# Sums of the down weights begin two pairs later in each up-projection

## The chip, the cores and the metric

The kernel runs on one core of one Trainium2 chip. The metric is device time in microseconds, from start to end of one execution. Five engines work side by side, each strictly in the order of its own instruction queue: PE (TensorE, matrix products; its weight loads are shown apart as PEld), DVE (VectorE), ACT (ScalarE), POOL (GpSimd) and SP (SyncE, which here issues the DMA transfers). An instruction whose input is not there holds up all that stands behind it on its engine.

## What is computed

The reference is one inference step of a two-layer encoder for 1024 prompt rows and 128 sample rows (1152 in all) of width 1024. Each layer is an attention block, then a channel mixer ("conv FFN"). The change lies in the channel mixer, which both layers run:

```python
def conv_ffn(h, prev, w_up, conv_w, conv_b, w_down):
    u = h @ w_up                          # 1024 -> 5632 columns
    ue = jnp.concatenate([prev, u], axis=1)
    y = conv_b
    for tap in range(CONV_W):             # 3 taps over positions
        y = y + conv_w[tap] * ue[:, tap:tap + T]
    a, g = jnp.split(y, 2, axis=-1)       # 2816 columns each
    out = (jax.nn.gelu(g) * a) @ w_down   # 2816 -> 1024
    return out, ue[:, T:]
```

## The kernel before

A float32 operand is held as a rounded part and a remainder ("hi" and "lo", made by `split`: an ACT cast at line 177, then a DVE subtraction at line 188), and each product is made of three matmuls.

**The up-projection (`ffn`, line 1213 on).** The 5632 columns are 44 blocks of 128. Block j of `a` and block j of `g` form pair j, with j from 0 to 21. Pairs 0 and 1 are `plain`: ordinary products. Pairs 2 to 21 are `spair`: each 2x2 block product is done with seven products instead of eight (`products`, line 1152), which needs sums of the two weights and sums of the input. The sums of the input are made once for each layer, by `tsums`, in the program between the plain pairs and pair 2: nine tiles go through a ring of three buffers; each is loaded (line 1131), POOL makes two subtractions (lines 1135, 1136), DVE two more (1137, 1138), ACT and DVE split the results, and only then may the buffer take the next tile. The sums of a pair's weights are four POOL operations (lines 1177 to 1180), then split for PE. PE multiplies at line 1229; the results are taken out of PSUM by ACT (1188, 1197) and DVE (1190); then come the convolution taps (`conv_row`: ACT at 1318 and 1321, DVE at 1278 and 1323, POOL at 1287), the gelu (ACT, 1330) and the gate (POOL, 1331), whose result `actD` goes to DRAM.

**Work for the down-projection inside this loop.** The down-projection (`down`) also uses seven products, so it needs sums of activations and of the down weights, both put in DRAM ahead of time. `act_sums` (POOL at 1343 to 1346, then two `actS` stores at 1348) works in place on the two gate buffers after each odd pair, and the next writer of a gate buffer (DVE, 1323) must wait for the store. `weight_sums(m)`, for m from 0 to 10, works in place in a buffer of its own, `w0`: two loads (line 1354), POOL at 1355, 1356 and 1357, and two stores to `wT` (1358, 1359). There is one such buffer, so the loads of m wait for the stores of m-1. The list `wsum` says in which pair m is called; its index in the list is m.

**Other work in the loop of layer 0.** `ada` streams modulation weights through the same load buffers as the pairs (loads at 226, PE at 234), and after pair 2 a table is unrolled to DRAM by `skew_b`, 16 DRAM-to-DRAM copies (line 1673).

**What sets the order.** The kernel is traced in program order and a scheduler then fixes one order for each engine from its own estimate of times; `issue_after` adds a constraint. So an edit moves not only its own instructions.

Of the kernel before, what the change touches and what calls it, by code (L numbers as in the profile page):

```python
# [19 lines left out]
NFF = 22  # L20
# [82 lines left out]
class Trunk:  # L103
# [1140 lines left out]
    def ffn(self, l, xsrc, xdst, affs):  # L1244
# [150 lines left out]
            gated(j, ya, y[0])  # L1395

        self.pend = []
        wsum = [2, 3] + list(range(4, NFF - 1, 2))
        for j in range(NPL):
            plain(j)  # L1400
        self.take_w0(F32)
# [534 lines left out]
```

## Time and profile before

| | us |
|---|---|
| median of 3 runs (lowest, highest) | 2820.66 (2814.4, 2827.81) |
| the profiled execution | 2813.54 |
| its span, first to last instruction | 2811.8 |
| PE busy | 2657.6 (95%) |
| DVE busy | 2031.0 (72%) |
| ACT busy | 1393.4 (50%) |
| POOL busy | 1031.4 (37%) |

Times in the trace count from the start of the span. Layer 0's up-projection runs from about 480 to 1020, layer 1's from about 2010 to 2530. A share of busy time is an average over stages; which engine waits, and for what, is read stage by stage. In a row of the timeline the columns are start, duration, engine, line, operation, output<-input, size and count, and in brackets the idle time of the engine before it and what ended it. In a row of windows they are the stretch, its length, then busy time and number of instructions of PE, PEld, DVE, ACT and POOL, the clock granted to PE (1.00 is full), the busy share of the DMA engines and GB/s.

### The profile page before, as it was taken

Reading aid. Unit: us, or ns where it says so; the run is one execution under the profiler, and the core shown is the slowest. Engines: PE = TensorE matmul, PEld = TensorE weight load, DVE = VectorE, ACT = ScalarE, POOL = GpSimd, SP = SyncE. Lnnn points to the kernel's source line nnn. Section 1 sums busy time; section 2 is a strip of 40 time slices with the busy share of each in tenths; the row PEclk is TensorE's granted clock in tenths of the full one; section 3 lists DMA queues with packets and bytes.
Section 4 is the critical chain, followed back from the end, with each engine's and each line's share of the span. In section 5 each row is a group of like instructions: output and inputs, shape, how many; then the busy total and the mean of one; then the engine's idle time right before and its main releaser. Section 6 shows DMA issues by size and latency. Waiting matters only on the chain.

```text
span 2811.8 us, 47453 instructions
## 1 busy us (share of the span) xinstructions
PE 2657.6 (95%) x17134; PEld 2341.9 (83%) x17134; DVE 2031.0 (72%) x4010; ACT 1393.4 (50%) x2912; POOL 1031.4 (37%) x808
## 2 busy tenths in 40 slices
PE   7999889989999999998899999989989999999997
PEld 5887768889999997877798888867889999997775
DVE  4376767777777785679654677767888888885668
ACT  3475724443444344455636666663444444444554
POOL 2132523456555642112420122242465656542101
PEclk9999999999999999999999999999999999999998
DMA  8756444575565557675767467764453433347664
GB/s 296 222 163 190 141 131 158 186 275 198 190 206 201 186 169 245 199 246 194 279 205 266 114 162 197 215 193 142 156 189 112 143 134 130 132 145 249 199 211 151
DMA packets 252715, 528.59 MB, mean 188 GB/s; under 512 B 40032, under 2 KB 100400, under 8 KB 252480
## 3 DMA queue, kind: packets, MB, share of 16 engines
q1 hardware_dynamic: 252480, 525.56, 56.9%
q8 instruction: 135, 2.21, 0.3%
q14 instruction: 100, 0.82, 0.1%
HBM read 391.12 MB, written 143.77 MB: 190 GB/s over the span
## 4 chain that ended last, share of the span: by engine, by line
PE 69%; DVE 11%; DMA 10%; POOL 4%; issue 3%; ACT 3%; SPq 1%; DVEq 0%; POOLq 0%; ACTq 0%
PE PS L1229 26%; PE PS L1476 15%; PE PS L319 10%; PE PS L306 7%; PE PS L602 2%; PE PS L580 2%; DVE wl L188 2%; PE PS L234 2%; PE PS L551 1%; DMA w0f<-in_wdn_dram 1%; PE PS L293 1%; DMA actS<-F 1%; DMA ws<-in_adaw_dram 1%; DVE F L518 1%; PE PS L554 1%
## 5 line engine op out<-in xcount | busy, mean ns | idle before, releaser
L1229 PE MATMUL PS<-H,wh 128*128 128x256 f32 (+1 forms) x2624 | 408.6, 298 | 0.0
L1476 PE MATMUL PS<-wh,xa 128*128 128x512 f32 x1144 | 366.5, 400 | 17.5 <-ACT wh L177 6.4
L1229 PEld LDWEIGHTS PS<-H,wh 128*128 128x128 f32 x2624 | 373.1, 192 | 0.4 <-issue 0.4
L188 DVE TENSOR_TENSOR wl<-F,wh 128x512 fp32r<-128x512 f32 (+2 forms) x278 | 274.2, 996 | 31.6 <-ACT wh L177 29.1
L1190 DVE TENSOR_TENSOR F<-PS,F 128x320 f32<-128x320 f32 (+1 forms) x446 | 196.4, 450 | 130.3 <-PE PS L1229 129.2
L1476 PEld LDWEIGHTS PS<-wh,xa 128*128 128x128 f32 x1144 | 216.9, 190 | 74.4 <-ACT wh L177 12.4
L177 ACT CAST wh<-F 128x512 fp32r<-128x512 f32 (+2 forms) x278 | 163.7, 598 | 219.4 <-PE PS L1229 132.5
L1229 PE MATMUL PS<-H,wl 128*128 128x256 f32 (+1 forms) x1312 | 234.3, 301 | 22.2 <-ACT F L1197 15.8
L1476 PE MATMUL PS<-wl,xa 128*128 128x512 f32 x572 | 228.1, 400 | 0.4 <-DVE wl L188 0.4
L1229 PEld LDWEIGHTS PS<-H,wl 128*128 128x128 f32 x1312 | 196.7, 193 | 30.8 <-ACT F L1197 16.2
L1321 ACT ACTIVATE PS<-F 128x512 f32<-128x512 f32 x160 | 124.6, 779 | 187.6 <-DVE F L1323 107.2
L188 DVE TENSOR_TENSOR xa<-xa 128x640 fp32r<-128x640 f32 (+1 forms) x154 | 128.0, 836 | 122.2 <-ACT xa L177 121.1
L1229 PE MATMUL PS<-xa,wh 128*128 128x320 f32 (+1 forms) x1328 | 203.8, 296 | 0.0
L1331 POOL TENSOR_TENSOR F<-F 128x1152 f32<-128x1152 f32 x44 | 125.6, 2855 | 188.9 <-DVE F L1323 147.7
L177 ACT CAST xa<-xa 128x640 fp32r<-128x640 f32 (+1 forms) x154 | 104.0, 682 | 178.2 <-DMA xa<-actD 118.2
L1229 PEld LDWEIGHTS PS<-xa,wh 128*128 128x128 f32 x1328 | 186.3, 189 | 0.0
L177 ACT CAST wh<-ws 128x512 fp32r<-128x512 f32 (+1 forms) x153 | 104.3, 691 | 97.8 <-PE PS L1229 30.2
L1065 POOL TENSOR_TENSOR F<-F 128x1024 f32<-128x1024 f32 x24 | 58.6, 2443 | 227.8 <-PE PS L1042 95.1
L188 DVE TENSOR_TENSOR wl<-ws,wh 128x512 fp32r<-128x512 f32 (+1 forms) x135 | 135.7, 1011 | 8.4 <-ACT wh L177 7.9
L640 POOL TENSOR_TENSOR F<-F,x2r 64x512 f32<-64x512 f32 x62 | 79.4, 1281 | 168.2 <-DVE F L616 147.2
L319 PE MATMUL PS<-xa,H 128*128 128x512 f32 x504 | 133.3, 405 | 6.2 <-ACT xa L177 3.3
L306 PE MATMUL PS<-H,w0r 128*128 128x384 f32 (+1 forms) x720 | 138.3, 342 | 0.0
(349 smaller groups left out, 6384.2 us busy)
## 6 DMA issues: line engine op xcount, KB each, us to landing
ws<-in_adaw_dram SPq DMA_DIRECT2D x64, 512.0 KB
ws<-in_wup_dram SPq DMA_DIRECT2D x49, 512.0 KB
F<-in_adaw_dram SPq DMA_DIRECT2D x48, 512.0 KB
w0f<-in_wdn_dram SPq DMA_DIRECT2D x44, 512.0 KB
actS<-F SPq DMA_DIRECT2D x44, 512.0 KB
xa<-actS SPq DMA_DIRECT2D x88, 256.0 KB
F<-in_wup_dram SPq DMA_DIRECT2D x39, 512.0 KB
xa<-actD SPq DMA_DIRECT2D x66, 256.0 KB
```

The source lines that it names most:

```text
L177: nc.scalar.copy(out, in_)
L188: self.eng(el).tensor_sub(lo, src, hi.bitcast(F32))
L234: mm = nc.tensor.matmul(ps[32 * j : 32 * j + 32, hf * 256 : hf * 256 + 256], self.cT[:, k * 32 : k * 32 + 32], w[:, j * 256 : j * 256 + 25 ...
L306: mm = self.nc.tensor.matmul(out[:, 0:n], w[a][:, k * 128 : k * 128 + 128], H[:, p, k, s0 : s0 + n], start=i == 0, stop=i == 23)
L319: self.nc.tensor.matmul(out[:, 0:n], H[:, p, j * kn + k, t0 : t0 + 128], w[a][:, k * n : k * n + n], start=i == 0, stop=i == 23,)
L640: self.eng("v" if last else "p").tensor_mul(on[r, q], on[r, q], rb[r, :])
L1065: self.eng(er[0]).tensor_mul(xr, x, self.lng)
L1190: nc.vector.tensor_add(d, v(ps), a if len(a.shape) == 3 else v(a))
L1229: self.pairmm = nc.tensor.matmul(ps[:, 0:m], w[a][:, k * 128 : k * 128 + 128], x(p, k, n), start=start and c == 0, stop=c == 11, skip_grou ...
L1321: nc.scalar.activation(ps, u[:, 2 + o : 514 + o], AF.Identity, **aff)
L1331: nc.gpsimd.tensor_mul(yg, yg, ya)
L1476: self.downmm = nc.tensor.matmul(ps, a[p][:, i * 128 : i * 128 + 128], w[q], start=first and c == 0, stop=last and c == 2, skip_group_chec ...
```

## The change

The list `wsum` is replaced; nothing else.

```diff
@@ ffn @@
         self.pend = []
-        wsum = [2, 3] + list(range(4, NFF - 1, 2))
+        wsum = list(range(4, 9)) + list(range(10, NFF - 1, 2))
         for j in range(NPL):
             plain(j)
```

With NFF = 22 the list was 2, 3, 4, 6, 8, 10, ..., 20 and is now 4, 5, 6, 7, 8, 10, ..., 20. Both have eleven entries. Sums 0, 1 and 2 move from pairs 2, 3, 4 to pairs 4, 5, 6; sum 3 moves from pair 6 to pair 7; sums 4 to 10 stay. Pairs 2 and 3 lose their sums, pairs 5 and 7 gain one. This holds in both layers. Each sum moved is four DMAs on SP's queue (two loads of 512 KB, stores of 256 and 512 KB) and three POOL operations on 128x512.

What it does to the order is seen at two places.

POOL at the start of layer 0's up-projection, from the sixth tile of `tsums` on. Before (L1135 and L1136 are the tile subtractions, w0f is the buffer of the weight sums, L1331 is the gate of pair 0):

```order
L1135 TENSOR_TENSOR F<-F 128x4x64
L1136 TENSOR_TENSOR F<-F 128x4x64
L1355 TENSOR_TENSOR w0f<-w0f 128x512
L1331 TENSOR_TENSOR F<-F 128x1152
L1356 TENSOR_TENSOR w0f<-w0f 128x512
L1135 TENSOR_TENSOR F<-F 128x4x64 x3
L1357 TENSOR_TENSOR w0f<-w0f 128x512
L1136 TENSOR_TENSOR F<-F 128x4x64 x3
```

Now:

```order
L1135 TENSOR_TENSOR F<-F 128x4x64
L1287 TENSOR_TENSOR F<-F 128x8x2
L1136 TENSOR_TENSOR F<-F 128x4x64
L1331 TENSOR_TENSOR F<-F 128x1152
L1135 TENSOR_TENSOR F<-F 128x4x64 x2
L1136 TENSOR_TENSOR F<-F 128x4x64
L1135 TENSOR_TENSOR F<-F 128x4x64
L1136 TENSOR_TENSOR F<-F 128x4x64 x2
```

The three operations of sum 0 are gone from between the tile subtractions, and the second subtraction of one tile now stands ahead of the last tile. Layer 1 has the same rows at its start.

SP's queue in layer 0 from the second weight load of pair 3 (L1376) to the first of pair 4 (L1375); skb<-eb are the copies of the table, actS the activation sums. Before:

```order
L1376 DMA ws<-in_wup_dram 128x1024
L1354 DMA w0f<-in_wdn_dram 128x1024 x2
L226 DMA F<-in_adaw_dram 128x1024
L1673 DMA skb<-eb 128x1x768 x9
L1348 DMA actS<-F 128x1024
L1673 DMA skb<-eb 128x1x768 x2
L226 DMA ws<-in_adaw_dram 128x1024
L1358 DMA wT_104<-w0f 128x512
L1673 DMA skb<-eb 128x1x768
L1348 DMA actS<-F 128x1024
```

Now:

```order
L1376 DMA ws<-in_wup_dram 128x1024
L226 DMA F<-in_adaw_dram 128x1024
L1673 DMA skb<-eb 128x1x768 x9
L1348 DMA actS<-F 128x1024
L1673 DMA skb<-eb 128x1x768 x3
L1348 DMA actS<-F 128x1024
L226 DMA ws<-in_adaw_dram 128x1024
L1673 DMA skb<-eb 128x1x768
L226 DMA F<-in_adaw_dram 128x1024
L1673 DMA skb<-eb 128x1x768 x3
L226 DMA ws<-in_adaw_dram 128x1024
L1375 DMA ws<-in_wup_dram 128x1024
```

Both loads of sum 1 and its stores are gone from this stretch, and the two activation stores stand nearer to its start.

ACT in layer 0 from the gelu (L1330) that stood ahead of the first weight casts of pair 4 (L177 CAST wh<-ws) on, before:

```order
L1318 ACTIVATE F<-F 128x128
L1291 COPY F<-F 128x18
L1321 ACTIVATE PS<-F 128x512
L1330 ACTIVATE F<-F 128x1152
L177 CAST wh<-ws 128x512 x2
L177 CAST wh<-F 128x512
```

Now:

```order
L1318 ACTIVATE F<-F 128x128
L1291 COPY F<-F 128x18
L177 CAST wh<-ws 128x512 x2
L1321 ACTIVATE PS<-F 128x512
L177 CAST wh<-F 128x512 x2
L1318 ACTIVATE F<-F 128x128
```

The casts of pair 4's weights no longer stand behind the last convolution steps of pair 3 and its gelu.

## The prediction

> **What bounds the kernel now.** I read the page first, then the windows of the two up-projections, PE's waits in the opening of each, and there the timelines of POOL, DVE, ACT and SP. In the first fence are windows:
>
> ```profile
> 607.00:1010.00 403.00, 403.00 (x3159) 373.03 (x3160) 306.31 (x475) 169.49 (x320) 240.76 (x184) 1.00 0.58 196
> 2104.00:2530.00 426.00, 419.82 (x3127) 418.03 (x3125) 370.80 (x547) 198.51 (x376) 239.64 (x183) 1.00 0.39 134
> ...
> 533.80:540.64 6.84, 0.00 (x0) 0.00 (x1) 6.41 (x14) 6.01 (x12) 0.00 (x0) 0.79 0.49 154
> 540.64:581.80 41.16, 40.73 (x308) 38.26 (x312) 26.43 (x41) 13.42 (x26) 19.48 (x17) 0.95 0.80 274
> 581.80:584.08 2.28, 0.41 (x9) 0.01 (x1) 2.06 (x4) 0.05 (x1) 0.52 (x1) 1.00 1.06 385
> 584.08:593.60 9.52, 9.50 (x64) 8.28 (x64) 5.43 (x13) 2.18 (x5) 2.36 (x2) 0.82 1.01 371
> 593.60:597.83 4.23, 0.00 (x0) 0.00 (x0) 3.99 (x7) 4.23 (x8) 3.31 (x4) 0.75 0.83 315
> 597.83:612.00 14.17, 13.12 (x82) 12.31 (x83) 12.57 (x11) 4.38 (x9) 11.32 (x7) 0.83 0.51 165
> ...
> 2063.00:2072.00 9.00, 0.08 (x2) 0.04 (x1) 8.57 (x18) 7.32 (x15) 2.77 (x5) 0.72 0.56 203
> ```
>
> From 607 on layer 0 is bound by PE alone: 403.00 busy of 403.00 us. There nothing that POOL or the DMAs gain or lose reaches the end while PE stays fed. Layer 1 loses 6.2 us of 426. What is not PE's own time lies in the openings: in layer 0 three stops, at 533.8, 581.8 and 593.6, and in layer 1 one of 8.9 us at 2063. After each stop the clock is lower for some microseconds (0.95, 0.82, 0.83), which lengthens the matmuls. PE's waits in the opening of layer 0, and then of layer 1:
>
> ```profile
> PE PS L1229 <- ACT F L1197: 6.9, 1, 6.9
> PE PS L1229 <- DVE wl L188: 5.7, 3, 4.2
> PE PS L1229 <- DVE F L1190: 1.9, 1, 1.9
> ...
> PE PS L1229 <- ACT F L1197: 8.9, 1, 8.9
> PE PS L1229 <- DVE F L1190: 4.6, 5, 2.6
> ```
>
> **Term A, the opening of both layers.** PE stands at 533.8 because ACT's copy L1197 comes only at 540.17. It queues behind the last casts of the input sums, and those hang on POOL and DVE (timelines, layer 0):
>
> ```profile
> 516.29 1.48 POOL L1355 TENSOR_TENSOR w0f<-w0f 128x512 f32<-128x512 f32 x1
> 518.74 2.68 POOL L1331 TENSOR_TENSOR F<-F 128x1152 f32<-128x1152 f32 x1 [0.97 <-ACT F L1330]
> 521.38 1.47 POOL L1356 TENSOR_TENSOR w0f<-w0f 128x512 f32<-128x512 f32 x1
> 528.29 0.74 POOL L1135 TENSOR_TENSOR F<-F 128x256 f32<-128x256 f32 x1 [3.68 <-DVE F L1278]
> 528.99 1.29 POOL L1357 TENSOR_TENSOR w0f<-w0f 128x512 f32<-128x512 f32 x1
> 530.24 2.31 POOL L1136 TENSOR_TENSOR F<-F 128x256 f32<-128x256 f32 x3
> ...
> 516.53 1.52 DVE L1137 TENSOR_TENSOR F<-F 128x256 f32<-128x256 f32 x1
> 518.08 0.42 DVE L1138 TENSOR_TENSOR F<-F 128x256 f32<-128x256 f32 x1
> 518.99 4.15 DVE L188 TENSOR_TENSOR xa<-F,xa 128x256 fp32r<-128x256 f32 x2 [0.48 <-ACT xa L177]
> 523.06 0.96 DVE L188 TENSOR_TENSOR x2r<-F,x2r 128x256 fp32r<-128x256 f32 x1
> 531.01 0.94 DVE L1137 TENSOR_TENSOR F<-F 128x256 f32<-128x256 f32 x1 [0.82 <-POOL F L1136]
> ...
> 524.05 0.32 SPq L1131 DMA_DIRECT2D F<-hD  x1
> 540.17 0.69 ACT L1197 COPY F<-PS 128x320 f32<-128x320 f32 x2
> ```
>
> Two things are seen. While POOL runs L1355, a DVE subtraction of the size that takes 0.42 takes 1.52; and two such take 4.15, to 523.1, while POOL runs L1331 and then L1356. And the last tile is loaded at 524.05, when the subtraction of 523.06 (0.96 long) has freed its buffer. Without sum 0, DVE comes free after L1331, at 521.4 instead of about 522.9: 1.4 us sooner, and so does the last load. Its first subtraction then comes at about 526.9, L1357's 1.29 us behind it are gone, and one of the three L1136 (0.77 each) stands ahead now: POOL ends 1.4 + 1.3 + 0.8 = 3.5 us sooner. DVE, which works nearly without a pause from 524 to 538, follows by less: its start is 1.4 sooner, the pause of 0.82 goes, and of the long 0.96 at 523.06 some 0.2 goes too. That is 2.4, and ACT's chain to L1197 follows DVE one for one. Bounds: 0 (DVE and ACT take no less time in another order) and 4.2, the whole of 1.48 + 1.47 + 1.29. I take 2.4, since DVE is the later of the two. Layer 1 has the same operations and the longer stop: twice 2.4 = 4.8 us. Both stops stay over 4 us, so the low clock behind them stays.
>
> The Trainium skill, page "SBUF — State Buffer", section "SBUF: two separate sides", says that DVE and GpSimd share one pair of ports, and that whichever starts first holds it for a whole instruction, the other blocking. The rows of 1.52 and 4.15 agree. By that rule alone each of the three operations would be given back whole, 4.2 us a layer, and term A would be 8.5 us; it also holds for the same operations in pairs 5 and 7.
>
> **Term B, the crowded DMA of layer 0.** From about 555 to 595 the DMA engines are full. Windows, then SP's rows, then the chain of waits, then the sizes:
>
> ```profile
> 560.00:580.00 20.00, 19.57 (x149) 18.81 (x149) 16.18 (x21) 8.32 (x17) 12.64 (x11) 1.00 1.03 361
> 554.48 0.90 SPq L1354 DMA_DIRECT2D w0f<-in_wdn_dram  x2
> 556.53 9.00 SPq L1673 DMA_DIRECT2D skb<-eb  x9
> 583.19 0.33 SPq L1375 DMA_DIRECT2D ws<-in_wup_dram  x1
> 566.23 9.25 DMA actS<-F
> 575.50 0.76 DVE F L1323
> 583.53 0.50 DVE F L1190
> w0f<-in_wdn_dram SPq DMA_DIRECT2D x44, 512.0 KB
> wT<-w0f SPq DMA_DIRECT2D x22, 512.0 KB
> wT<-w0f SPq DMA_DIRECT2D x22, 256.0 KB
> ```
>
> Sum 1 is issued into this: 1024 + 512 + 256 = 1792 KB, 1.84 MB, at 361 GB/s 5.1 us of full DMA. Its two loads (2.9 us) stand ahead of everything. The activation store needs 9.25 us to land, so DVE's L1323 (the convolution of pair 2, into the buffer just stored) starts at 575.50, and PE's next evict L1190 waits in DVE's queue until 583.53: the second stop, 2.28 - 0.41 = 1.87 us. With term A's 2.4 and the 2.9 us the store lands about 5 us sooner, while PE arrives only 2.4 sooner. The slack of 2.9 covers the 1.87: the stop goes, and the slow stretch behind it (9.52 us at 0.82: 1.7 us) with it. Together 3.6 us. Bounds: 0 and 3.6.
>
> On that slow stretch the Trainium skill, page "TensorE: Matmul & The Clock Gate", section "What's actually happening", says the clock falls after an idle window of about 3.4 us. Here 0.82 follows a stop of 1.87 us, so the row and not the page is used; by the page this term would be 1.9.
>
> **Term C, the third stop.** At 593.6 PE waits for pair 4's weights. Their cast stands behind pair 3's last convolution steps and gelu; in the new order it stands ahead of them, so it is bound by the landing of the weights. These are issued at 583.19 after 1.84 MB less and with PE 2.4 us ahead; they wait also for a buffer that PE's ada matmuls free just before 581.8, so I reckon issue at 579, landing at 584 to 585 (the crowd is through by then), cast and split by 586.5. PE would be there at 593.6 - 2.4 - 1.87 - 1.7 = 587.6. So the stop of 4.23 goes, with the slow clock behind it (14.17 us at 0.83: 2.4) and the small waits in it (14.17 - 13.12 = 1.05): 7.7 us. Bounds: 0 and 7.7. I take it whole, since the weights come 1 us before PE; that margin is thin.
>
> **Term D, what pairs 5 and 7 pay.** The four sums moved cost three POOL operations each, 4.2 to 5 us, in pairs where POOL is busy 240.76 of 403.00 and 239.64 of 426.00, and 1.84 MB of DMA at shares of 0.58 and 0.39. In layer 0 PE's queue covers this. In layer 1 a sum makes POOL wait for its loads:
>
> ```profile
> 2175.93 7.02 DMA w0f<-in_wdn_dram
> 2152.55 1.43 PE L1229 MATMUL PS<-xa,wl 128*128 128x320 f32 x4 [2.64 <-DVE F L1190]
> DMA w0f<-in_wdn_dram: 42.3, 10
> ```
>
> The load takes 7 us, POOL waited ten times for it, 42.3 us in all, and once (at 2152) PE lost 2.64 behind it. Where such a pair has no activation sums to do, as pairs 5 and 7, I take 0.5 each: +1 us. Bounds 0 and 2 x 2.64 = 5.3. SP's queue and the single buffer are covered: load 7, POOL 5 and store about 3 us are 15 of the 20 to 25 us that a pair takes (403.00 us hold about 16).
>
> **Sum.** -4.8 - 3.6 - 7.7 + 1.0 = -15.1 us. On the profiled execution's own 2813.54 that gives 2798.4; the median of the runs shown, 2820.66, lies 7.1 above it, so I predict a median of 2805.6.
>
> **Rivals.** First: only term A comes true. The third stop stays, its cause only renamed: pair 4's weights land later than reckoned, or the ada matmul whose weights are loaded inside the crowd now stands ahead of PE's products and PE waits for it. For it: full DMA at 1.03, and a margin of 1 us. Then -4.8 plus part of B, about -6: 2815.
>
> Second: the change does nothing that reaches the end, as another chain of DVE work (6.41 of 6.84 us busy in the first stop) takes the place of each one shortened: 0 to +2, 2821 to 2823.
>
> Third, the other side: sums in five pairs running, through one buffer. POOL stands at L1355 until the loads land, and behind it, in order, stand the gate L1331, the activation sums and the next pair's weight sums. If each of pairs 4 to 7 in both layers pays what 2152 shows, 2.64 and as much again as its clock costs (about 1.4), that is 8 x 4.0 = 32 us against the gain of 15: +17, 2838. It decides once these stops pass 29 us. Against it: before, sums ran in pairs 2, 3 and 4 in a row too, and layer 0 from 607 on stops for none of its sums.
>
> **How the numbers follow.** The forecast (A, B, C) 0.50, of which 0.08 falls short of 14 us; only A 0.30, of which 0.02 passes it; nothing 0.06; the slow rival 0.14. 0.5% of the median is 14 us, about what a measurement of this kernel can tell from no change. Faster: 0.42 + 0.02 = 0.44; same: 0.08 + 0.28 + 0.06 = 0.42; slower 0.14. The forecast alone: 2800 to 2812. The range reaches below to the sum with A at its upper bound (-18.8) and the spread of a median (4), 2797, and above past no change to 2826, half the way into the slow rival; 0.17 is left out.
>
> **What will show it.** Right: the stop ahead of L1197 falls to about 4.5 us in layer 0 and 6.5 in layer 1; the last tile load comes 1.4 us sooner after the first; the activation store lands by 571; no stop of PE over 1 us between there and 700. Wrong: a PE wait on an ada load or on line 188 near 585 (term C fails), L1197 as late as before (term A), or in layer 1 between 2100 and 2250 waits on L1190 that pass 10 us (the slow rival).

## The result and the profile after

| | before | after |
|---|---|---|
| median of 21 runs, us | 2821.82 | 2812.03 |
| lowest, us | 2814.27 | 2801.26 |
| ratio of the times | | 0.9968, 95% interval 0.9956 to 0.998 |

The change gains 9.0 us (5.6 to 12.4 by the interval). One of the 21 executions of the changed kernel, the one that was profiled with them, took 6333.7 us; it stands outside the ratio, and the profile after is read from two later executions of the same kernel (2822.73 us and, on another occasion, 2809.2 us with a span of 2807.2).

The windows of the two up-projections, each from its first L1229 to the first L1476 of the down-projection; before:

```profile
530.42:1054.05 523.63, 503.95 (x3890) 468.18 (x3889) 396.26 (x611) 220.76 (x415) 286.74 (x222) 0.98 0.59 202
2059.70:2531.31 471.61, 454.42 (x3362) 451.85 (x3361) 409.75 (x604) 218.24 (x416) 275.19 (x214) 0.99 0.40 138
```

After, first and second execution:

```profile
536.54:1054.02 517.48, 501.30 (x3890) 465.49 (x3889) 402.09 (x613) 218.86 (x415) 290.13 (x223) 0.99 0.61 207
2068.41:2536.36 467.95, 451.59 (x3362) 449.30 (x3361) 412.66 (x603) 218.09 (x415) 278.48 (x214) 0.99 0.41 141
```

```profile
537.53:1055.41 517.88, 502.13 (x3890) 466.36 (x3889) 399.86 (x612) 217.77 (x412) 288.59 (x221) 0.99 0.61 207
2061.59:2526.77 465.18, 452.27 (x3361) 449.97 (x3360) 410.71 (x601) 217.67 (x415) 277.13 (x213) 0.99 0.41 142
```

The second number is the length. Layer 0 loses 6.2 and 5.8 us of its 523.63, layer 1 3.7 and 6.4 of its 471.61: 9.8 and 12.2 us together. These lengths are used below because the rest of the program, whose work is the same, scatters more than the change is worth: 1816.6 us in the execution of before, 1835.4 and 1824.1 in these two.

PE's stops in the openings after (first execution, timeline of PE, the rows with an idle time ahead), layer 0 and then layer 1:

```profile
545.63 1.43 PE L1229 MATMUL PS<-H,wl 128*128 128x320 f32 x4 [5.74 <-ACT F L1197]
573.49 0.86 PE L1229 MATMUL PS<-xa,wl 128*128 128x320 f32 x4 [0.78 <-DVE wl L188]
587.99 0.64 PE L234 MATMUL PS<-F,C 128*32 128x256 f32 x8 [0.27 <-DMA F<-in_adaw_dram]
633.22 0.85 PE L1229 MATMUL PS<-xa,wl 128*128 128x320 f32 x4 [0.65 <-DVE F L1190]
642.51 0.87 PE L1229 MATMUL PS<-x2r,wl 128*128 128x320 f32 x4 [1.30 <-DVE F L1190]
658.48 0.75 PE L1229 MATMUL PS<-H,wl 128*128 128x256 f32 x4 [0.86 <-ACT F L1197]
...
2079.21 1.43 PE L1229 MATMUL PS<-H,wl 128*128 128x320 f32 x4 [7.44 <-ACT F L1197]
2110.85 0.86 PE L1229 MATMUL PS<-xa,wl 128*128 128x320 f32 x4 [0.90 <-DVE F L1190]
2157.28 0.86 PE L1229 MATMUL PS<-xa,wl 128*128 128x320 f32 x4 [1.85 <-DVE F L1190]
2203.71 0.86 PE L1229 MATMUL PS<-xa,wl 128*128 128x320 f32 x4 [1.41 <-DVE F L1190]
```

The opening stops are shorter (6.87 to 5.74, 8.92 to 7.44). The second and third stop of layer 0, 1.87 and 4.25 us before, are gone. New in this execution are three stops in layer 0 between 633 and 659, in pairs 5 and 6, and the longer one of pair 7 in layer 1 (2203; 0.48 before). Placed against the same matmul before, layer 0 is 11.7 us ahead early in pair 5 and 8.2 ahead from pair 9 on (second execution: 9.6 and 6.8): about 30% of the gain is given back.

### The profile page after: what moved, and what is told of

It reads as the page before. It is cut to its first block, busy times and chain, and to the rows that moved or that the text cites. A ratio compares the mean times of both kernels' runs of the same rounds, so it can differ in the third digit from the quotient of the medians.

```text
span 6331.7 us, 47437 instructions
## 1 busy us (share of the span) xinstructions
PE 6286.0 (99%) x17134; PEld 4896.8 (77%) x17134; DVE 1877.5 (30%) x4010; ACT 1418.0 (22%) x2912; POOL 964.0 (15%) x808
## 4 chain that ended last, share of the span: by engine, by line
PE 99%; DVE 0%; DMA 0%; issue 0%; ACT 0%; SPq 0%; ACTq 0%
PE PS L1229 39%; PE PS L1476 18%; PE PS L319 13%; PE PS L306 12%; PE PS L602 4%; PE PS L580 3%; PE PS L234 2%; PE PS L551 2%; PE PS L554 2%; PE PS L293 1%; PE PS L1042 1%; PE PS L729 1%; PE PS L694 1%; PE PS L720 0%; PE PS L628 0%; PE PS L1697 0%
## 5 line engine op out<-in xcount | busy, mean ns | idle before, releaser
L1229 PE MATMUL PS<-H,wh 128*128 128x256 f32 (+1 forms) x2624 | 950.3, 566 | 0.0
L1229 PEld LDWEIGHTS PS<-H,wh 128*128 128x128 f32 x2624 | 869.7, 398 | 32.2 <-issue 1.2
L1476 PE MATMUL PS<-wh,xa 128*128 128x512 f32 x1144 | 733.9, 751 | 0.0
L1190 DVE TENSOR_TENSOR F<-PS,F 128x320 f32<-128x320 f32 (+1 forms) x446 | 203.6, 458 | 1341.4 <-PE PS L1229 1333.0
L1476 PEld LDWEIGHTS PS<-wh,xa 128*128 128x128 f32 x1144 | 370.8, 325 | 234.9 <-issue 221.7
L1229 PE MATMUL PS<-H,wl 128*128 128x320 f32 (+1 forms) x1312 | 516.4, 571 | 0.0
L1229 PE MATMUL PS<-xa,wh 128*128 128x320 f32 (+1 forms) x1328 | 481.2, 564 | 0.0
L1229 PEld LDWEIGHTS PS<-H,wl 128*128 128x128 f32 x1312 | 445.3, 390 | 29.0 <-ACT F L1318 11.9
L1229 PEld LDWEIGHTS PS<-xa,wh 128*128 128x128 f32 x1328 | 438.2, 396 | 17.7
L1476 PE MATMUL PS<-wl,xa 128*128 128x512 f32 x572 | 428.9, 751 | 0.0
L177 ACT CAST wh<-F 128x512 fp32r<-128x512 f32 (+2 forms) x278 | 163.3, 598 | 1054.0 <-PE PS L1229 719.1
L188 DVE TENSOR_TENSOR wl<-F,wh 128x512 fp32r<-128x512 f32 (+2 forms) x278 | 197.7, 720 | 464.1 <-ACT wh L177 463.1
L306 PE MATMUL PS<-H,wh 128*128 128x384 f32 (+1 forms) x672 | 320.4, 686 | 0.0
L306 PEld LDWEIGHTS PS<-H,w0r 128*128 128x128 f32 x720 | 250.6, 356 | 66.8 <-issue 56.9
L306 PEld LDWEIGHTS PS<-H,wh 128*128 128x128 f32 x672 | 234.8, 355 | 60.6 <-issue 53.4
L1476 PEld LDWEIGHTS PS<-wl,xa 128*128 128x128 f32 x572 | 184.5, 323 | 117.1 <-issue 107.6
L319 PE MATMUL PS<-wh,H 128*128 128x512 f32 (+1 forms) x468 | 273.9, 736 | 0.0
L1229 PE MATMUL PS<-xa,wl 128*128 128x320 f32 (+1 forms) x664 | 260.4, 569 | 0.0
```

The costliest lines, as they stand in the source:

```text
L177: nc.scalar.copy(out, in_)
L188: self.eng(el).tensor_sub(lo, src, hi.bitcast(F32))
L306: mm = self.nc.tensor.matmul(out[:, 0:n], w[a][:, k * 128 : k * 128 + 128], H[:, p, k, s0 : s0 + n], start=i == 0, stop=i == 23)
L319: self.nc.tensor.matmul(out[:, 0:n], H[:, p, j * kn + k, t0 : t0 + 128], w[a][:, k * n : k * n + n], start=i == 0, stop=i == 23,)
L1190: nc.vector.tensor_add(d, v(ps), a if len(a.shape) == 3 else v(a))
L1229: self.pairmm = nc.tensor.matmul(ps[:, 0:m], w[a][:, k * 128 : k * 128 + 128], x(p, k, n), start=start and c == 0, stop=c == 11, skip_grou ...
```

## The experiments

Each kernel was timed beside the kernel before. Lengths are of one profiled execution, from first L1229 to first L1476; the down-projection and all else stay out.

| kernel | sums in pairs | layer 0, us | layer 1, us | ratio to before (95%) |
|---|---|---|---|---|
| before | 2, 3, 4, 6, 8, ... | 523.63 | 471.61 | |
| changed, two executions | 4 to 8, 10, 12, ... | 517.48, 517.88 | 467.95, 465.18 | 0.9978 (0.9961, 0.9995), 0.9966 (0.9947, 0.9985) |
| layer 0 alone | new list in layer 0 | 515.88 | 470.17 | 0.9971 (0.9954, 0.9987) |
| pair 2 alone | 3, 4, 5, 6, 8, ... | 523.01 | 470.02 | 0.9997 (0.9982, 1.0012) |
| pair 3 alone | 2, 4, 5, 6, 8, ... | 518.07 | 465.96 | 0.9984 (0.9969, 0.9999) |
| traffic back in pair 3 | changed | 521.70 | 466.42 | 0.9961 (0.9944, 0.9978) |
| the same, doubled | changed | 521.22 | 468.87 | 0.9969 (0.9955, 0.9982) |
| POOL work back in pair 3 | changed | 513.88 | 466.18 | 0.9948 (0.9929, 0.9966) |
| pair 5 free | 4, 6 to 10, 12, ... | 512.31 | 470.70 | 0.9949 (0.993, 0.9967) |
| late | 10 to 20 | 517.25 | 469.75 | 0.9961 (0.9945, 0.9978) |
| split list | per layer, below | 512.97 | 467.43 | 0.9957 (0.994, 0.9973) |
| second split list | per layer, below | 514.13 | 466.29 | 0.9948 (0.9931, 0.9965) |

The intervals are 8 to 11 us wide, so a term of 2 to 4 us is read from the trace and not from them.

### The changed kernel once more

No edit.

> The changed kernel again, for a profile that can be read. Its measured gain is 9 to 10 us where the prediction's sum gave 15.1. Theory S (layer 0 fell short: the third stop, term C, stays in part because pair 4's weights land later than reckoned): a PE stop of 2 us or more stands between 575 and 600 of layer 0, and PE's loss in layer 1's opening is 2 to 3 us less than before. Theory L (layer 0 gives all 13.7 us of A, B and C, and layer 1 gives 4 to 5 us back in pairs 4 to 7): no PE stop over 1 us between 545 and 700, and PE waits on L1190 between 2100 and 2250 that add up to 4 us more than before.

Its ratio is 0.9978 (0.9961 to 0.9995). Neither theory holds as put. No stop of 2 us stands between 575 and 600, so the third stop did not stay (against S); but layer 0 stops for over 1 us at 642 (against L). What is short in layer 0 was lost later than S said, in pairs 5 and 6.

### The new list in layer 0 alone

```diff
-wsum = list(range(4, 9)) + list(range(10, NFF - 1, 2))
+wsum = (list(range(4, 9)) + list(range(10, NFF - 1, 2))) if l == 0 else [2, 3] + list(range(4, NFF - 1, 2))
```

> The new list in layer 0 alone; layer 1 keeps the old one. Theory S: about -6 us against before (A 2.4 and B 3.6), layer 1's share being -3. Theory L: -13 to -14 us, 4 to 5 more than with the change in both layers.

The ratio is 0.9971, -8.2 us (-3.7 to -13.0): it does not tell -6 from -13. The lengths do: layer 0 gained 7.8 us, less than L's 13, and layer 1, with the old list, was 470.17 where before had 471.61. That 1.4 us is scatter of the same code: its stop in pair 5 was 2.44 us and no slow clock followed, before it was 2.64 and one did.

### Only pair 2 loses its sum

```diff
-wsum = list(range(4, 9)) + list(range(10, NFF - 1, 2))
+wsum = [3, 4, 5] + list(range(6, NFF - 1, 2))
```

> Sums begin in pairs 3, 4, 5, 6, 8, ... in both layers: pair 2 alone loses its sum, so the three POOL operations are gone from the opening as in the change, and sum traffic stays in pair 3. Term A says -4.8 us (2.4 in each layer: the stop at 533.8 falls from 6.8 to 4.4, that at 2063 from 8.9 to 6.5), less up to 1 for pair 5; by the port rule alone -8.5; the rival in which another chain of DVE work takes the place of the one shortened says 0, with both stops as long as before.

The ratio, 0.9997 (-5.1 to +3.4 us), excludes the -8.5 of the port rule and nothing else. PE's rows of layer 0:

```profile
543.08 1.43 PE L1229 MATMUL PS<-H,wl 128*128 128x320 f32 x4 [4.92 <-ACT F L1197]
571.12 0.86 PE L1229 MATMUL PS<-xa,wl 128*128 128x320 f32 x4 [0.72 <-DVE wl L188]
587.13 0.86 PE L1229 MATMUL PS<-x2r,wl 128*128 128x320 f32 x4 [1.97 <-DVE F L1190]
600.88 1.44 PE L1229 MATMUL PS<-H,wl 128*128 128x320 f32 x4 [4.25 <-DVE wl L188]
```

The first stop fell from 6.87 to 4.92, in layer 1 from 8.92 to 7.09: 1.95 and 1.83. In all the kernels without a sum in pair 2 it is 4.5 to 5.7 in layer 0 and 5.4 to 7.4 in layer 1 (means 4.9 and 6.6); in the two with one 6.9 and 7.2, and where layer 1 has one 8.6 to 9.1. So term A's stops are as forecast, some 2.1 and 2.3 us less. Not all of it arrives: 0.3 is lost at the next small stop (0.72 here, 0.43 before), and the second and third stop stay, the third to the hundredth of a microsecond. Layer 0 gains 0.6 in all, layer 1 1.6.

### Only pair 3 loses its sum

```diff
-wsum = list(range(4, 9)) + list(range(10, NFF - 1, 2))
+wsum = [2, 4, 5] + list(range(6, NFF - 1, 2))
```

> Sums begin in pairs 2, 4, 5, 6, 8, ... in both layers: pair 3 alone loses its sum, the opening stays as before. Terms B and C without A: in layer 0 1792 KB less in the crowded DMA, the activation store lands 3 us sooner, the second stop (1.87 us) goes, the third is ACT's order only. If B and C hold without A: -9 to -11 us. Theory S: -2 to -4, with a stop of 2 us or more left for pair 4's weights. Rival, the opening carries everything: 0.

Layer 0 of this kernel:

```profile
547.22 1.44 PE L1229 MATMUL PS<-H,wl 128*128 128x320 f32 x4 [7.15 <-ACT F L1197]
590.34 0.64 PE L234 MATMUL PS<-F,C 128*32 128x256 f32 x8 [0.91 <-DMA F<-in_adaw_dram]
644.01 0.85 PE L1229 MATMUL PS<-x2r,wl 128*128 128x320 f32 x4 [1.29 <-DVE F L1190]
```

The first stop is the old one (7.15) and the second and third are gone without term A's help. That stretch gains 10.2 us, that of 1.29 is one of the new stops of the changed kernel and gives some back, and layer 0 is 5.6 shorter. Terms B and C hang on pair 3 alone, and they are nearly whole. The ratio, 0.9984 (-0.3 to -8.7 us), is less than the 11.2 us by which the two layers of the one profile are shorter. This is the only kernel whose lengths and times part, and it is left open: the profile's layer 1 (465.96) may have been a lucky one.

### What in pair 3: the traffic or the POOL work

The first kernel puts the two loads and two stores of one sum back into pair 3 of layer 0, without POOL's three operations; the second puts those three operations back (on a weight tile that is there anyway), without a transfer. The third has the traffic twice.

Both call `weight_sums` in pair 3 of layer 0 with m = -1 (the first then moves the tiles of sum 0):

```diff
-                if i == 2 and j in wsum:
+                if i == 2 and (j in wsum or (l, j) == (0, 3)):
```

Traffic, in `weight_sums` (the two other POOL lines likewise):

```diff
-            nc.gpsimd.tensor_sub(b12, b22, b12)
+            m < 0 or nc.gpsimd.tensor_sub(b12, b22, b12)
```

POOL work (the two stores likewise):

```diff
-                nc.sync.dma_start(self.w0[i], I["wdn"][l, 2 * m + i])
+                m < 0 or nc.sync.dma_start(self.w0[i], I["wdn"][l, 2 * m + i])
```

> The changed kernel with the traffic of one sum put back in pair 3 of layer 0: two loads of 512 KB into the sum buffer and stores of 256 and 512 KB from it (overwritten later by the real sum), no POOL work. Against before, the changed kernel stands at -6 to -9 us. Theory of traffic (the crowded DMA made the second and third stop): the stops come back, 1.9 us before pair 3's last products and 2 us or more for pair 4's weights, and the kernel loses 6 to 9 us against the changed one, so 0 to -2 against before. Theory of order (ACT's place for pair 4's casts made the third stop; the casts stay ahead of the gelu here): at most the second stop comes back with its low clock, and the kernel keeps -4 or more.

> The changed kernel with the three POOL operations of one sum put back in pair 3 of layer 0, on a weight tile already there, no DMA; the order of the other engines is the same as in the changed kernel. Theory of traffic: 0 to +1 us against the changed kernel (-6 to -9 against before), the openings as there. Rival, POOL's three operations (4.2 us, and what they hold up on DVE) made the stops: +4 us or more, with a stop on L1190 or L188 before pair 4.

> The changed kernel with the traffic of two sums in pair 3 of layer 0 (four loads, four stores, 3.67 MB, no POOL work). With one sum's traffic the trace showed the stops of before again (1.55 and 4.25 us), but the times did not tell it from the changed kernel. Theory of traffic: 5 us more of full DMA, so the stops before pair 4 grow to 8 us or more and the kernel comes to 0 to +5 against before. Rival, the stops answer to order alone: as with one, -7 to -10 against before.

PE with one sum's traffic, and the DVE step that waits for the activation store:

```profile
585.91 0.86 PE L1229 MATMUL PS<-x2r,wl 128*128 128x320 f32 x4 [1.55 <-DVE F L1190]
598.91 1.43 PE L1229 MATMUL PS<-H,wl 128*128 128x320 f32 x4 [4.25 <-DVE wl L188]
...
577.34 0.75 DVE L1323 SCALAR_TENSOR_TENSOR F<-F,PS 128x512 f32<-128x512 f32 x1 [4.09 <-DMA actS<-F]
```

PE with the POOL work, between 545 and 645 (its stop of 0.96 is one of pair 5's):

```profile
583.95 0.64 PE L234 MATMUL PS<-F,C 128*32 128x256 f32 x8 [0.42 <-DMA F<-in_adaw_dram]
637.50 0.85 PE L1229 MATMUL PS<-x2r,wl 128*128 128x320 f32 x4 [0.96 <-DVE F L1190]
```

The same DVE step, and the cast of pair 4's weights, in the changed kernel; then that cast with the traffic:

```profile
578.73 0.75 DVE L1323 SCALAR_TENSOR_TENSOR F<-F,PS 128x512 f32<-128x512 f32 x1 [1.32 <-DMA actS<-F]
593.38 1.14 ACT L177 CAST wh<-ws 128x512 fp32r<-128x512 f32 x2 [0.27 <-DMA ws<-in_wup_dram]
```

```profile
595.15 1.13 ACT L177 CAST wh<-ws 128x512 fp32r<-128x512 f32 x2
596.94 1.15 ACT L1330 ACTIVATE F<-F 128x1152 f32<-128x1152 f32 x1
```

In the trace both stops come back with the traffic (1.55 and 4.25); with the POOL work neither does, and nothing over 0.5 us stands in their place. The kernel with the POOL work keeps the order of PE, DVE and ACT, so that rival falls cleanly: layer 0 is 513.88 and the ratio 0.9948.

The traffic kernel differs by more than its transfers, for the scheduler also gave DVE and ACT another order before pair 4. What each of the two does can be read, counted from each execution's first L1229 (536.54 changed, 533.04 with the traffic). The DVE step that waits for the store comes at 42.2 and 44.3. Pair 4's first weight load is issued at 50.4 and 50.0, and the last of its 16 DMA completions in the trace is at 56.8 and 61.2: in the fuller DMA it lands 4.4 us later. From there to pair 4's first product it takes 2.4 us in the changed kernel and 4.7 with the traffic (5.9 before). The cast still stands ahead of the gelu (L1330), but with one more round of L1321, L1318 and L1291 ahead of it, and DVE's split stands behind more convolution steps and takes 1.76, beside POOL, in place of 0.68. So of the 6.7 us by which pair 4 begins later (65.9 for 59.2), some 4.4 are the traffic and some 2.3 the order.

Doubled, the traffic does not double the stop. The scheduler put the second pair of loads near the end of the crowd, and the cast behind the gelu again; the second stop was 0.94 and the third 5.32 where 8 or more was expected, and layer 0 came to 521.22. And the times do not show what the trace shows: both traffic kernels lose 4 us of layer 0's length against the changed one, and both ratios (0.9961, 0.9969) lie where the changed kernel's do. The intervals, 10 us wide, allow 4 us; they do not confirm it. It is only 4 because neither traffic kernel stops in pairs 5 and 6, where the changed one gives some of its lead back.

### Pair 5 without a sum

```diff
-wsum = list(range(4, 9)) + list(range(10, NFF - 1, 2))
+wsum = [4, 6, 7, 8, 9] + list(range(10, NFF - 1, 2))
```

> Sums in pairs 4, 6, 7, 8, 9, 10, 12, ..., 20: sum 1 leaves pair 5 for pair 6, and so on. In the changed kernel layer 0 stops 0.65, 1.30 and 0.87 us between 95 and 122 us after its first L1229, and its second weight load of pair 6 is issued behind an activation store that waits for POOL, whose activation sums stand between sum 1's three operations. Theory of the queue: without sum 1 there, the stop of 1.30 and its neighbours go and the kernel gains 2 to 3 us over the changed one, -9 to -12 against before. Rival, any sum in these pairs costs the same: 0 against the changed one.

The changed kernel, DVE, then POOL, then SP:

```profile
627.41 1.45 DVE L188 TENSOR_TENSOR wl<-ws,wh 128x512 fp32r<-128x512 f32 x1
...
630.33 1.77 DVE L188 TENSOR_TENSOR wl<-ws,wh 128x512 fp32r<-128x512 f32 x1
632.03 0.73 DVE L1323 SCALAR_TENSOR_TENSOR F<-F,PS 128x512 f32<-128x512 f32 x1
...
640.31 1.74 DVE L188 TENSOR_TENSOR wl<-ws,wh 128x512 fp32r<-128x512 f32 x1
641.98 1.54 DVE L1190 TENSOR_TENSOR F<-PS,F 128x320 f32<-128x320 f32 x4
...
626.98 1.33 POOL L1345 TENSOR_TENSOR F<-F 128x512 f32<-128x512 f32 x1
...
628.90 1.37 POOL L1357 TENSOR_TENSOR w0f<-w0f 128x512 f32<-128x512 f32 x1
630.24 1.32 POOL L1346 TENSOR_TENSOR F<-F 128x512 f32<-128x512 f32 x1
...
640.24 1.27 POOL L1177 TENSOR_TENSOR F<-F 128x512 f32<-128x512 f32 x1 [8.06 <-DMA F<-in_wup_dram]
...
632.13 0.33 SPq L226 DMA_DIRECT2D ws<-in_adaw_dram  x1
632.51 0.45 SPq L1348 DMA_DIRECT2D actS<-F  x1
633.06 0.38 SPq L1376 DMA_DIRECT2D F<-in_wup_dram  x1
```

With pair 5 free, the same DVE steps, and POOL's last activation sum:

```profile
619.32 0.68 DVE L188 TENSOR_TENSOR wl<-ws,wh 128x512 fp32r<-128x512 f32 x1
...
620.32 0.75 DVE L1323 SCALAR_TENSOR_TENSOR F<-F,PS 128x512 f32<-128x512 f32 x1
...
621.24 0.69 DVE L188 TENSOR_TENSOR wl<-ws,wh 128x512 fp32r<-128x512 f32 x1
...
617.66 1.28 POOL L1346 TENSOR_TENSOR F<-F 128x512 f32<-128x512 f32 x1
```

With a sum in pair 5 POOL's activation sums last until 631.6 (L1357 is that sum, between the activation sums L1345 and L1346), and beside them DVE's splits L188 take 1.45 and 1.77. With pair 5 free POOL's last activation sum ends at 618.9, the same splits take 0.68 and 0.69, and DVE's L1323 follows its evict by 1.3 us, not by 5.0. In the changed kernel the chain of L1323 that begins there at 632.03 and one more slow split, 1.74 beside POOL's L1177, hold up the evict L1190 until 641.98, and PE has its stop of 1.30. In the second execution that last split began before L1177 and took 0.68, and PE's stop at the same matmul was 0.24.

The second thing is SP's queue. An ada load (632.13) waits for the buffer that the slow split of 630.33 frees at 632.10; behind it stand the activation store (632.51) and the next weight load (633.06), and POOL waits 8.06 us for that load; from there the chain of waits leads to the stop of 0.86 at 658.

With pair 5 free PE stops for neither L1190 nor L1197 between 566 and 720, and layer 0 is 512.31, 5.4 shorter than the mean of the changed kernel's two. The theory was right on the place and on the stops, and wrong on what holds the queue: POOL's activation sums were done 0.5 us before DVE's split. The cause at the head is DVE beside POOL, and the queue carries it on. Layer 1 gave 4 us back (470.70): pair 7 stopped 2.58 us there.

A sum in pair 5 does not cost this by itself. Pair 2 alone and both traffic kernels have one and do not stop in pairs 5 and 6. PE comes there 6 to 10 us later after its first L1229 than in the changed kernel, and POOL has the sum behind the activation sums (pair 2 alone: the last of them, L1346, at 618.40, the sum's L1355 at 624.70). No run tells which of the two spares them.

### All sums late

```diff
-wsum = list(range(4, 9)) + list(range(10, NFF - 1, 2))
+wsum = list(range(10, NFF - 1))
```

> Sums in pairs 10 to 20, one in each: none in the opening pairs of either layer. Theory: the gains of the opening stay (layer 0 about -11 us by pair 4, layer 1 about -4), and the stops of pairs 5 to 7 go, so -12 to -15 us against before, if a sum in each of eleven pairs running in layer 1 costs under 0.3 us each. Rival, running pairs pay: each odd pair with a sum costs layer 1 0.9 us as pair 7 does in the changed kernel, five more of them take 4.5 back, -8 to -9.

PE's waits on this kernel's evict line, in layer 0 and in layer 1:

```profile
PE PS L1229 <- DVE F L1190: 7.9, 2, 6.6
...
PE PS L1229 <- DVE F L1190: 8.9, 6, 2.5
```

The rival holds, in another form. Layer 0 keeps 12 us to pair 18, then stops 1.28 in pair 20 and 6.61 in pair 21. The last sum is over at 991.5, and the stop of 6.61 ends at 1040: its chain of waits leads over the down-projection's first loads, not over a sum. Layer 1 is 10.4 ahead in pair 8 and has no stop over 0.5 us between its first (5.36) and there, so without sums near it the stop of 2.64 in pair 5 does not exist; the pairs from 9 on, with eleven sums in a row, then cost all but 1.9 us of that, in six stops of 0.6 to 2.5.

### A list for each layer

```diff
-wsum = list(range(4, 9)) + list(range(10, NFF - 1, 2))
+wsum = list(range(8, 19)) if l == 0 else [5, 7, 8, 9, 11, 12, 13, 15, 16, 17, 19]
```

> A list for each layer: layer 0 sums in pairs 8 to 18, layer 1 in 5, 7, 8, 9, 11, 12, 13, 15, 16, 17, 19, mostly pairs in which no activation sums run. Theory: layer 0 keeps what the kernel with sums in pairs 10 to 20 showed up to its last pairs (-12 us) and, with no sum in pairs 19 to 21, not its stop of 6.61 us there; layer 1 loses the stop of 1.6 to 2.6 us in pair 5, which followed a sum in pair 4 beside activation sums, and a sum in an odd pair costs 0.5 us or less, so -5 to -8 there: -17 to -20 together. Rival, a sum costs layer 1 1 us wherever it stands: -12 to -14 together.

> The changed kernel again beside these two, as their measure: -7 to -10 us against before, the same stops in layer 0 as in its first profile (5 to 6, 0.8, 0.7, 1.3 and 0.9 us, none before pair 4), 7 and 1.9 us in layer 1.

And with the second list for layer 1, `[5, 6, 8, 9, 10, 12, 13, 14, 16, 17, 20]`:

> Layer 0 as in the split list (pairs 8 to 18), layer 1 in 5, 6, 8, 9, 10, 12, 13, 14, 16, 17, 20. In the split list layer 1 stopped 2.18, 1.25 and 2.43 us in pairs 7, 11 and 15, and nowhere in 5, 9, 13 and 17; the new list leaves 7, 11, 15 and 19 free. Theory (a sum costs layer 1 most in pairs 7, 11, 15, where a gate buffer's activation sums follow at once): those stops go, layer 0 -10 to -11 and layer 1 -7 to -9, together -17 to -19. Rival (the stop follows the sum into whichever pair has it or the next): stops of 1.5 us or more remain in three pairs, and it is worth what the split list is, -11 to -15.

PE's waits in layer 1, first and second list:

```profile
PE PS L1229 <- DVE F L1190: 5.9, 3, 2.4
```

```profile
PE PS L1229 <- DVE F L1190: 6.1, 5, 2.2
```

Layer 0 comes near what was expected: 512.97 and 514.13, that is -10.7 for -12 and -9.5 for -10 to -11. Layer 1 does not: with the first list it stops 2.18, 1.25 and 2.43 us in pairs 7, 11 and 15, with the second 2.23, 1.50 and 1.23 in pairs 5, 9 and 13. The stop follows the list, so the rival of the second run holds, with a third stop a little under its 1.5. In these two lists the stops stand in odd pairs that have a sum and whose next, even pair has one too. That rule was read from them afterwards, and other kernels break it: before and with pair 5 free, layer 1 stops 2.64 and 1.63 in a pair 5 without a sum.

The second list has the best ratio of those shown, 0.9948 (0.9931 to 0.9965), with that of the POOL work (0.9948) and of the free pair 5 (0.9949); the interval overlaps that of the changed kernel beside the first list (0.9947 to 0.9985), so that it beats the changed kernel is not shown.

The changed kernel repeated its stops only in part. In layer 0 it had 4.85 and 0.88 first, then three that were not expected before pair 4 (1.52 and 0.72 on ada loads, 0.62 on L188), and in place of the three in pairs 5 and 6 only 0.83 and 1.03, both in pair 6. In layer 1 it had 6.34, 1.68 and 1.34.

## Why the prediction was right, and where it was not

The median, 2812.03, lies in the range (2797 to 2826) and 6.4 us above the forecast of 2805.6. The range is wide enough to hold the median of before as well, so it is the sum that is tested here. The direction and the main cause are right; 6 of the 15.1 us are missing. For layer 0 the terms are measured by the time from the first L1229 to the same matmul, before against the changed kernel's two executions.

**Term A (-4.8).** The stops fell by 2.1 and 2.3 us as means over all kernels, for 2.4 each, and the low clock behind them stays, as said. The working was near, not exact: the last tile load came 0.4 and 1.3 us sooner against PE's first product in layer 0, for 1.4, and DVE's last split 0.6 and 1.5 sooner. "ACT's chain to L1197 follows DVE one for one" misses 0.5 us that ACT gained besides, so the size came out right in part by luck. Layer 0 keeps 0.8 and 1.5 of it past the next small stop, which grew by 0.4; layer 1 is 3.2 and 4.4 ahead at the start of pair 4.

**Terms B and C (-11.3).** Together they measure -10.9 and -8.1 in the changed kernel and -10.2 with pair 3 alone. B's chain is right, its margin was thinner than reckoned: the store landed 2.9 us sooner after the first L1229 in the first execution and PE came 0.8 sooner, and the 2.1 between them cover the 1.87. In the second it is 3.1 and 1.5; there PE waited 1.52 and 0.72 for ada loads instead. That is the first rival in small, and it is what is missing. C's thin margin held: the cast at 593.38 waited 0.27 for the weights, and PE lost at most 0.62 there. C's reason is right as far as it goes: counted from the first L1229, pair 4's weights land 4.7 us sooner than before (56.8 for 61.5), and from there to the first product it takes 3.5 us less (2.4 for 5.9), which is the new order.

**Term D (+1.0).** This is the step that failed. "In layer 0 PE's queue covers this" does not hold for pairs 5 and 6: they give back 3.4 and 2.8 us. I looked for the price in POOL's and the DMA's shares of busy time; it stood in what is beside and behind the three operations. Sum 1 falls among the activation sums, DVE's splits beside them take twice their time and more, and an ada load that waits for one of them holds up SP's queue, and with it the next weights. The first of these is the rule of the Trainium skill that the prediction named (page "SBUF — State Buffer", section "SBUF: two separate sides": a DVE step with two inputs in SBUF and a GpSimd one lock a pair of ports against each other for a whole instruction), and it said there that it holds for pairs 5 and 7 too; 0.68 against 1.45 and 1.77 agrees, and the sum left it out. "Where such a pair has no activation sums to do, as pairs 5 and 7, I take 0.5 each" is wrong for layer 1 as well: the chain of the changed kernel there has sum and activation sums together.

```profile
2180.87 6.70 DMA w0f<-in_wdn_dram
...
2199.15 2.61 DMA actS<-F
...
2201.85 1.41 DVE F L1323 x2
2203.26 0.41 DVE F L1190
2203.71 0.41 PE PS L1229
```

After the sum's load POOL does nine operations, then comes the store, then DVE's step, behind it the evict, and PE: the slow rival's mechanism, in pair 7 alone, in place of the 4.0 in each of eight pairs. Five executions here have this list in layer 1, with the same order: pair 7's stop is 1.41, 1.34 and 1.48 in three of them, and 0.45 and 0.64 in the two with the traffic, near the 0.48 of before, so it is not paid each time. Against it stands that pair 5's stop of 2.64 became 1.85 and 1.68 with no slow clock behind it, which no term had.

So by layer 0: A -0.8 and -1.5, B and C -10.9 and -8.1, D +3.4 and +2.8, and its last pairs +2.1 and +1.1 (the stops of pair 21 add up to 2.8 to 6.6 us from kernel to kernel, whatever the list's start): -6.2 and -5.7, as measured. Of the rivals, "only term A" and "nothing" fall with the second and third stop, the slow one with its price.

## What to carry to other kernels

Work that is off the bottleneck is moved for what stands beside and behind it, not for its busy time: here a sum's 1.84 MB in a full DMA stretch, with the order that came with it, was worth 7 to 9 us of the trace (the traffic kernel against the changed one, in pair 5), the three POOL operations there nothing, and a whole sum among the activation sums about 3 us. After such a move, ask at the new place which operations it comes between, which DVE steps run beside them, and what stands in the queue behind those. And price a short stop in steps, since one of 2 us costs as much again or nothing in clock.

## What the runs showed of the hardware

The slow clock comes in whole windows. Before, layer 0, three windows cut to where the clock was low:

```profile
537.75:544.55 6.80, 3.91 (x15) 3.91 (x16) 6.26 (x9) 3.94 (x8) 0.36 (x3) 0.50 0.31 93
585.55:588.93 3.38, 3.38 (x17) 3.38 (x17) 0.49 (x1) 0.78 (x1) 0.67 (x1) 0.50 1.00 387
595.80:602.60 6.80, 4.77 (x19) 4.77 (x20) 6.74 (x7) 4.47 (x9) 4.73 (x4) 0.50 0.34 121
```

The clock is 0.50, never between, and its stretches are one, two or three times 3.41 us. They begin 1.9 to 4.7 us after a stop begins. In the thirteen profiles, over the lengths of the table, none of 82 stops of 0.5 to 1.54 us had one, 19 of 40 from there to 3.02 us, and all 32 from 3.03 us on. That is what windows of 3.41 us would give that run on their own and slow the clock for the next one once enough of one was idle: a stop of 1.5 to 3 us may or may not fall into one window with that much. Laid over the windows that the slow stretches mark, all 46 stops with 1.9 us or more inside one window had a slow stretch, none of 92 with up to 1.51 us had, and 5 of the 16 between. So the limit lies between 1.5 and 1.9 us. The Trainium skill, page "TensorE: Matmul & The Clock Gate", section "What's actually happening", has the free-running window of 3413 ns and the two states, and the rows agree; it has the clock fall after an idle window of about 3.4 us, and here a stop of 1.87 us was enough. It also bears on the scatter: the same code, layer 1 before and in the kernel with the new list in layer 0 alone, paid a window behind 2.64 us and none behind 2.44.
